# Four of eight attention gates moved into half-size products, and two sums moved between engines, in a hybrid decoder layer

## The chip, the cores and the metric

The kernel runs on one core of one Trainium2 chip. The metric is the time of one execution on the device in microseconds (us); lower is better. The core's engines run side by side and wait for each other by semaphores: TensorE (PE) multiplies matrices, VectorE (DVE) and GpSimd (POOL) do elementwise work, ScalarE (ACT) evaluates functions and copies, SyncE (SP) issues most DMAs. PE writes its products into PSUM banks, from which DVE and ACT read them.

## The reference

One decoder layer on 1024 tokens with 1024 channels, float32. A single projection of the normalized input feeds two token mixers; their outputs are projected, merged by gates, projected again, added to the input and normalized.

```python
h = rmsnorm(x, norm_g)
proj = h @ w_in
(g_q, g_k, g_v, g_gate, g_rank,
 s_q, s_k, s_v, s_gate, m_logits) = jnp.split(proj, SPLIT_IDX, axis=-1)
...
o_gla = rmsnorm(o_gla, gla_norm_g).reshape(B, T, GLA_DV) * jax.nn.silu(g_gate)
y_a = o_gla @ w_pa
o_sb = stick_breaking(s_q, s_k, s_v)          # 8 heads of 128
o_sb = o_sb.reshape(B, T, SB_WIDTH) * jax.nn.silu(s_gate)
y_b = o_sb @ w_pb
gates = jax.nn.sigmoid(m_logits + b_gate).reshape(B, T, N_BRANCH, D_MODEL)
merged = gates[:, :, 0] * y_a + gates[:, :, 1] * y_b
x = x + merged @ w_o
return rmsnorm(x, final_g)
```

Stick-breaking attention works on 128-query blocks against their causal key prefix: `log1m = log_sigmoid(-z)`, a reversed running sum over the keys gives `between`, and the weights are `exp(log_sigmoid(z) + between)`, strictly causal. The gate that this text follows most is `silu(s_gate)`, one 128-channel slice per attention head.

## The kernel before

Every float32 operand of a product is split into a high part, rounded to the fast float32 format by ACT (`split`, line 165), and a low part, the difference, by DVE (line 166). Each product is then three matmuls of 128 x 512: high by high, high by low, low by high.

The kernel runs in stages, in this order in time:

1. *Start and V* (0 to about 116 us). Normalization of x block by block (`norm_a`, `norm_b`, lines 386 to 399, with ACT's square, a small DVE instruction and POOL's power), transposes into the four quarters `hq`, and the value projections in `proj_n` (line 209). The first block's order on ACT and DVE is written out by hand (lines 424 to 455).
2. *Pairs with decay* (about 116 to 270). `Pairs` (line 69) works through a list of 28 jobs (lines 623 to 627). A job (`pair_job`, line 234) multiplies the two half matrices of hidden states by 256 columns of `w_in` with seven products of half size (Winograd's scheme) in place of eight: seven units of 12 matmuls (lines 269 to 272), the differences of the weights by POOL (lines 244 to 247), splits by ACT and DVE, and for each of four output parts an eviction. The first 22 units stand between the steps of the GLA decay (`djobs`, line 692); the next 31 between steps that load `w_pb` and `w_o`, form the differences `t_sum` on DVE and store them to `d_t` for the last stages (`tjobs`, line 729). `GLA_AT` = 53 is the number of units ahead of GLA. The jobs for GLA's q and k read the decay factors `d_e` from DRAM (line 558).
3. *GLA with pairs* (about 270 to 715). 32 steps of chunked linear attention, four units in each (line 877), the rest of the pair jobs beside them: stick-breaking q and k, the merge gates.
4. *Attention* (about 736 to 1015). 64 steps (head h, block i), lines 1088 to 1102. `scores` runs two steps ahead: three matmuls per piece, two sigmoids on ACT, a scan and a product on DVE (lines 963 and 967), a mask on POOL (line 964). `turn` transposes the block's weights on PE and splits them (near parts `at`, and `af` for the far half); `values(h, g)` multiplies them by v once for each half of the queries and evicts with the gate read from `d_sg` (lines 986 to 1004). Beside them runs a line of *filler units* (`Line`, line 55, and lines 1073 to 1081): a unit is a whole product of 24 matmuls (`proj_t`, line 197). First come 16 gate units (`gate`, line 1053: eight heads, two halves of the tokens, evicted by `silu`, line 567), then 16 units of `w_pa` (`pa`, line 1059). `SB_PLAN` says how many units run in step i before and after the transposes: one at 3, 6 and 7, so three a head; two units run ahead of the attention and six behind it.
5. *Branch output and merge* (about 1060 to 1125). 28 items (u, i) of 12 matmuls: seven half-size products (`PRODUCTS`, line 1231) of the attention output with `w_pb`. `a_merge` (line 1274) gates and adds into the merged blocks A11, A22, A12, A21. `parts` and `loads` (lines 1300 to 1313) say after which item k a weight or block is split (`his` by ACT, `los` by DVE) and loaded.
6. *Last projection* (about 1125 to 1219). 28 items (u, t) of 12 matmuls with `w_o`, the residual add, the squares and the final scaling; the loop at line 1423 goes on with the same k from 28. Its products need the sums S1 to S4 of the merged blocks (`sums`, line 1144), which POOL forms here (lines 1342 and 1438).

Outside the hand-ordered parts (`manual_schedule`) the framework's planner sets the order of instructions on each engine ahead of time by its own costs, in the order of the program where it can; each engine then runs its list in order.

Of the kernel before, what the change touches and what calls it, by code (L numbers as in the profile page):

```python
# [34 lines left out]

SB_PLAN = [(0, 0), (0, 0), (0, 0), (1, 0), (0, 0), (0, 0), (1, 0), (0, 1)]
# [9 lines left out]
GLA_AT = 53  # L46
# [57 lines left out]
def hybrid_layer(ctx: ExitStack, tc: tile.TileContext, x, norm_g, w_in, w_up, b_dec,  # L104
# [35 lines left out]
    d_s = {nm: dram_set("s" + nm, 2, [P, 2, HALF]) for nm in ("S3", "S4", "A22")}  # L140
# [220 lines left out]
    with tc.tile_pool(name="p0", bufs=3, reuse_waits="tile") as p0:  # L361
# [62 lines left out]
        with tc.manual_schedule(engines={mybir.EngineType.Activation, mybir.EngineType.DVE}):  # L424
            norm_a(0)
            (raw0, hi0, lo0), (raw1, hi1, lo1) = ws0
            norm_b(0, 0)
            norm_b(0, 1)
            xs = by_parity(xss[0])
            pts = []  # L430
            for g in range(2):
                pt = ps.tile([P, HALF], F32, tag="tr", name="tr")
                for j in range(4):
                    nc.tensor.transpose(pt[:, j * P:(j + 1) * P], xs[:, g, j], ident)
                pts.append(pt.rearrange("p (a b) -> p a b", a=4))
                nc.scalar.activation(hq[0, g][0][:, :, 0:P], pts[g], AF.Copy)
            nc.vector.tensor_copy(hi0, raw0)
            keep_warm(WARM[1])
            norm_a(1)
            for g in range(2):  # L440
                nc.vector.tensor_sub(hq[0, g][1][:, :, 0:P], pts[g], hq[0, g][0][:, :, 0:P].bitcast(F32))
            nc.vector.tensor_sub(lo0, raw0, hi0.bitcast(F32))
            nc.scalar.activation(hi1, raw1, AF.Copy)
            norm_b(1, 0)
            nc.vector.tensor_sub(lo1, raw1, hi1.bitcast(F32))
            norm_b(1, 1)
            ws0 = [w[1:] for w in ws0]
            for tb in range(1, NT):
                if tb + 1 < NT:
                    norm_a(tb + 1)  # L450
                turn_x(tb)
                if tb + 1 < NT:
                    norm_b(tb + 1)
                first_v(tb - 1)
            first_v(NT - 1)
# [136 lines left out]

    def gv_pair(h):
# [22 lines left out]
    def gla_qk(i):  # L616
# [10 lines left out]
                  [merge_pair(C_MB, i, d_gb) for i in range(4)] + [merge_pair(C_MA, 3, d_ga)], late)  # L627
# [83 lines left out]
    def t_load(k):  # L711
        wt[k] = tq.tile([P, 4, HALF], F32, tag="t", name="t")
        for two in range(2):
            rows = slice((2 * (k % 4) + two) * P, (2 * (k % 4) + two + 1) * P)
            if k < 4:
                for e in range(2):
                    nc.sync.dma_start(wt[k][:, 2 * two + e].rearrange("p (i c) -> p i c", c=P),
                                      w_pb[rows].rearrange("p (i e c) -> p e i c", e=2, c=P)[:, e])
            else:
                nc.sync.dma_start(wt[k][:, 2 * two:2 * two + 2], w_o[rows].rearrange("p (h c) -> p h c", h=2))  # L720
# [5 lines left out]
    def t_store(k):  # L726
        nc.sync.dma_start(d_t[k][:], wt[k])
# [360 lines left out]
    for s, (h, i) in enumerate(steps):  # L1088
        if i % 2 == 0 and s + 4 < len(steps):
            h2, i2 = steps[s + 4]  # L1090
            load_q(h2, i2 // 2)
        if i == 1 and h + 1 < SB_H:
            load_head(h + 1)
        if s + 2 < len(steps):
            scores(*steps[s + 2])
        st.run(SB_PLAN[i][0])
        turn(h, i)
        st.run(SB_PLAN[i][1])
        if i == 0 and s:
            values(h - 1, 1)  # L1100
        elif i == 5:
            values(h, 0)
    values(SB_H - 1, 1)
# [40 lines left out]
    def sums(pre, js, nms):  # L1144

        for j in js:
            for nm in nms:
                x1, x2_, fn, where = {"S1": ("A21", "A22", ALU.add, None), "S3": ("A11", "A21", ALU.subtract, "A21"),
                                      "S2": ("S1", "A11", ALU.subtract, "A11"),
                                      "S4": ("A12", "S2", ALU.subtract, "A12")}[nm]  # L1150
                dst = oraw[pre + where, j] if where else mo_tile("A22" if pre == "" else "N", j)
                nc.gpsimd.tensor_tensor(dst, oraw[pre + x1, j], oraw[pre + x2_, j], op=fn)
# [61 lines left out]
    sums("b", range(3), ("S1", "S3", "S2"))  # L1214
# [5 lines left out]
    sums("b", [3], ("S1", "S3", "S2"))  # L1220
# [3 lines left out]
    sums("b", ALL, ("S4",))  # L1224
# [68 lines left out]
    def y_load(n, t):  # L1293
        ys[n, t] = (sw.tile([P, D], F32, tag=("wh", "wl")[t % 2], name="y") if n == 0 else
                    py[0].tile([P, D], F32, tag="y", name="y"))
        r0 = n * HALF + t * P
        nc.sync.dma_start(ys[n, t], x2[r0:r0 + P, :])
# [14 lines left out]
    loads = {6: ("bB22", "tt"), 10: ("bT4",), 14: ("B11",), 16: ("B21", "tt"), 24: ("T2",), 26: ("T1",),  # L1312
             28: ("B22", "tt"), 34: ("S4",), 36: ("T3",), 39: ("S3", "tt"), 41: ("T4",), 43: ("A22",)}
# [16 lines left out]
    for k, it in enumerate(items):  # L1330
# [9 lines left out]
        if k >= 24:  # L1340
            y_load(0, k - 24)
            sums("", [k - 24], ("S1", "S3", "S2"))
# [15 lines left out]
    def add(n, t, J, bank):  # L1358
        nc.vector.tensor_add(ys[n, t][:, half(J)], bank, ys[n, t][:, half(J)])

    def square(n, t, J):
# [3 lines left out]
        nc.scalar.activation(junk, ys[n, t][:, half(J)], AF.Square, accum_out=ssq[:, i, J:J + 1])  # L1365
# [12 lines left out]
    def put(n, t, eng, J):  # L1378
        r0 = n * HALF + t * P
        eng.dma_start(o2[r0:r0 + P, half(J)], ys[n, t][:, half(J)])  # L1380

    def scale(n, t, J):
        y = ys[n, t][:, half(J)]
# [15 lines left out]
    def evict_c(u, t):  # L1399
# [4 lines left out]
        elif u == 5:  # L1404
            nc.vector.tensor_mul(ys[1, t][:, half(1)], ys[1, t][:, half(1)], fg[:, half(1)])
        elif u == 6:
            scale(1, t, 0)
            put(1, t, nc.sync, 0)
            nc.scalar.activation(ys[1, t][:, half(1)], ys[1, t][:, half(1)], AF.Copy, scale=pre[1, t][:, 1:2])
# [13 lines left out]
    for k, it in enumerate(items):  # L1423
# [6 lines left out]
        if 3 <= k < 7:  # L1430
            for nm in ("S4", "S3"):
                nc.sync.dma_start(d_s[nm][(k - 3) // 2][:, (k - 3) % 2], oraw[nm, k - 3])
            for nm in ("S4", "S3") if k == 6 else ():
                for j in range(4):
                    del oraw[nm, j]
        los(28 + k)
        if k < 4:
            sums("", [k], ("S4",))
# [4 lines left out]
        if k == 9:  # L1443
            mo_ctx.close()
            po.append(ctx.enter_context(tc.tile_pool(name="po", bufs=1, side="right", reuse_waits="tile")))
            py.append(ctx.enter_context(tc.tile_pool(name="py", bufs=4, reuse_waits="tile")))
            for t in range(4):
                y_load(1, t)
# [26 lines left out]
```

## Time and profile before

| What | Value |
|---|---|
| Median of three runs | 1220.27 us (1218.0 to 1220.41) |
| Profiled execution | 1220.52 us |
| Its span, first to last instruction | 1218.8 us |
| Mean granted PE clock | 0.992 |
| ACT busy | 556.1 us (46%) |
| POOL busy | 343.0 us (28%) |
| DMA moved | 249.77 MB, 205 GB/s on the mean |

Busy time is the union of an engine's instructions; a matmul's record includes the end of its pipeline, so neighbouring records overlap and the distance from start to start is its true price. "Idle before" names the instruction that the engine waited for. A granted clock of 1.00 is full speed. In the views by line, the columns are the group's count, its busy time, the mean of one in ns, and the idle time before it with what ended it. In the views by time they are start, duration, engine, line and names, and in brackets the idle time before and its cause.

### The profile page before, as it was taken

What the parts mean: (1) busy time and instruction counts of PE and PEld (TensorE: products, weight loads), DVE (VectorE), ACT (ScalarE), POOL (GpSimd) and SP (SyncE); (2) the same over time, 40 slices, a digit from 0 to 9 for tenths busy, and PEclk for the clock granted to TensorE, in tenths of its full rate; (3) what the DMA queues carried; (4) which work ended last, traced back from release to release, by engine and by line L of the source; (5) the groups of instructions that cost most, each with busy time, mean ns of one, the idle gap of its engine ahead of it and who ended that gap; (6) DMA issues with size and microseconds to landing.
All of it is one profiled execution on the core that took longest, in us unless ns stands there. A gap on an engine that the chain in (4) does not pass through costs nothing.

```text
span 1218.8 us, 17307 instructions
## 1 busy us (share of the span) xinstructions
PE 1190.8 (98%) x6087; PEld 1000.3 (82%) x6087; DVE 849.3 (70%) x1323; ACT 556.1 (46%) x1079; POOL 343.0 (28%) x319
## 2 busy tenths in 40 slices
PE   8999999999999999999999999999999999999797
PEld 8999878877888888888888887888887888788586
DVE  5575876786757667867666528777677874579876
ACT  5344663234335445444444325554456553374243
POOL 1495523142422322422423202111121111602601
PEclk9999999999999999999999999999999999999899
DMA  7544349976656646656655187545877547649562
GB/s 278 186 142 141 147 168 343 373 276 199 198 156 195 190 146 208 212 189 218 209 165 170 65 276 241 179 161 180 286 265 245 179 141 276 212 160 301 172 240 105
DMA packets 205652, 249.77 MB, mean 205 GB/s; under 512 B 12503, under 2 KB 141549, under 8 KB 203005
## 3 DMA queue, kind: packets, MB, share of 16 engines
q1 hardware_dynamic: 204988, 247.62, 61.7%
q8 instruction: 48, 0.79, 0.3%
q10 hardware_dynamic: 576, 1.05, 0.2%
q14 instruction: 40, 0.32, 0.1%
HBM read 155.30 MB, written 93.32 MB: 204 GB/s over the span
## 4 chain that ended last, share of the span: by engine, by line
PE 79%; DVE 9%; DMA 6%; ACT 3%; issue 2%; SPq 1%; POOL 0%; ACTq 0%; DVEq 0%; POOLq 0%
PE pp L270 12%; PE pp L272 12%; PE pp L271 12%; PE pp L223 8%; PE pp L204 4%; PE pp L205 4%; PE pp L206 4%; DMA f<-d_e 2%; PE av L1002 1%; PE z L955 1%; PE av L1001 1%; PE av L1000 1%; PE tr L979 1%; DMA raw<-in_w_in_dram 1%; PE z L957 1%
## 5 line engine op out<-in xcount | busy, mean ns | idle before, releaser
L964 POOL TENSOR_SCALAR_AFFINE_SELECT be<-be 128x128 f32<-128x128 f32 x64 | 40.4, 633 | 232.3 <-ACT be L960 221.1
L166 DVE TENSOR_TENSOR wl<-tt,wh 128x1024 fp32r<-128x1024 f32 x56 | 70.2, 1253 | 50.4 <-ACT wh L165 50.0
L244 POOL TENSOR_TENSOR tt<-raw 128x512 f32<-128x512 f32 x28 | 39.2, 1400 | 212.9 <-DVE wl L166 208.6
L309 DVE TENSOR_TENSOR f<-pp,f 128x512 f32<-128x512 f32 x84 | 57.7, 688 | 58.8 <-PE pp L272 58.1
L963 DVE TENSOR_TENSOR_SCAN eb<-eb,m 128x128 f32<-128x128 f32 (+3 forms) x64 | 86.5, 1353 | 9.5 <-ACT eb L959 9.5
L165 ACT ACTIVATE wh<-tt 128x1024 fp32r<-128x1024 f32 x56 | 59.3, 1059 | 68.8 <-PE pp L271 68.2
L165 ACT ACTIVATE wh<-raw 128x1024 fp32r<-128x1024 f32 x47 | 49.7, 1060 | 80.7 <-PE pp L271 39.5
L166 DVE TENSOR_TENSOR wl<-raw,wh 128x1024 fp32r<-128x1024 f32 x47 | 67.9, 1445 | 25.0 <-ACT wh L165 20.1
L276 ACT ACTIVATE f<-pp 128x512 f32<-128x512 f32 x84 | 49.6, 591 | 71.9 <-PE pp L272 70.5
L231 POOL TENSOR_TENSOR r<-r,nhalf 128x1 f32<-128x1 f32 x40 | 24.3, 607 | 188.5 <-DVE r L230 178.3
L959 ACT ACTIVATE eb<-z 128x384 f32<-128x384 f32 (+4 forms) x96 | 49.0, 511 | 36.7 <-issue 23.9
L967 DVE TENSOR_TENSOR be<-be,eb 128x128 f32<-128x128 f32 (+3 forms) x64 | 48.8, 763 | 3.2
L960 ACT ACTIVATE be<-z 128x384 f32<-128x384 f32 (+4 forms) x96 | 49.4, 515 | 0.0
L270 PE MATMUL pp<-ha11h,wh 128*128 128x512 f32 x112 | 44.8, 400 | 2.6 <-ACT wh L165 2.6
L270 PE MATMUL pp<-S3h,wh 128*128 128x512 f32 x112 | 45.0, 401 | 0.0
L270 PE MATMUL pp<-ha22h,wh 128*128 128x512 f32 x112 | 44.5, 397 | 0.2 <-DVE f L309 0.2
L270 PE MATMUL pp<-ha12h,wh 128*128 128x512 f32 x112 | 44.5, 397 | 0.0
L270 PE MATMUL pp<-S1h,wh 128*128 128x512 f32 x112 | 44.5, 397 | 0.0
L271 PE MATMUL pp<-S3l,wh 128*128 128x512 f32 x112 | 44.1, 394 | 0.0
L272 PE MATMUL pp<-S3h,wl 128*128 128x512 f32 x112 | 44.1, 394 | 0.0
L270 PE MATMUL pp<-S4h,dh 128*128 128x512 f32 x112 | 44.0, 392 | 0.0
L270 PE MATMUL pp<-S2h,wh 128*128 128x512 f32 x112 | 43.9, 392 | 0.0
(510 smaller groups left out, 4007.9 us busy)
## 6 DMA issues: line engine op xcount, KB each, us to landing
raw<-in_w_in_dram SPq DMA_DIRECT2D x31, 1024.0 KB, 6.4
d_v<-o SPq DMA_DIRECT2D x32, 256.0 KB, 3.0
d_gv<-o SPq DMA_DIRECT2D x32, 256.0 KB, 4.0
d_t<-t SPq DMA_DIRECT2D x8, 1024.0 KB, 5.5
v<-d_gv SPq DMA_DIRECT2D x32, 256.0 KB, 3.3
d_ogl<-o SPq DMA_DIRECT2D x64, 128.0 KB, 2.5
d_q<-o SPq DMA_DIRECT2D x16, 512.0 KB, 3.9
d_k<-o SPq DMA_DIRECT2D x16, 512.0 KB, 4.1
```

What stands on the lines that cost most here:

```text
L165: nc.scalar.activation(hi, src, AF.Copy)
L166: eng.tensor_sub(lo, src, hi.bitcast(F32))
L223: nc.tensor.matmul(pt[:, 0:n], *ops[kb][i], start=k == 0, stop=k == 3 * KB - 1)
L270: nc.tensor.matmul(pt, bh[:, j], ah[:, j], start=first and j == 0, stop=False, skip_group_check=True)
L271: nc.tensor.matmul(pt, bh[:, j], al[:, j], start=False, stop=False, skip_group_check=True)
L272: nc.tensor.matmul(pt, bl[:, j], ah[:, j], start=False, stop=j == 3, skip_group_check=True)
L276: nc.scalar.activation(t[nm], t[bank], AF.Copy)
L309: nc.vector.tensor_add(add, bank, add)
L959: nc.scalar.activation(om[:, osl], zt[:, 0:w], AF.Sigmoid, scale=-inv_sqrt)
L960: nc.scalar.activation(be[:, osl], zt[:, 0:w], AF.Sigmoid, scale=inv_sqrt)
L963: nc.vector.tensor_tensor_scan(rest, rest, m1[:, off:T][:, ::-1], 1.0, op0=ALU.mult, op1=ALU.max)
L967: nc.vector.tensor_mul(be[:, off:T], be[:, off:T], om[:, off + 1:T + 1])
```

## The change

There are six parts.

- The gates of heads 0 to 3 are no longer filler units. Two more pair jobs, `sg_pair(0)` and `sg_pair(1)`, form them (30 jobs in all), behind the q and k jobs; they evict by `silu` into the same `d_sg`. The filler line keeps the gates of heads 4 to 7 and all of `pa`.
- `SB_PLAN` now puts one filler unit at steps 0 and 6 of each head, ahead of the transposes. `values(h - 1, 1)` moves from step 0 to step 2, and both value products stand ahead of the step's transposes.
- `GLA_AT` goes from 53 to 70, and the weight sums of stage 2 start every 5 units instead of every 2.7; loads and stores are issued in halves.
- In the last projection the sums S1 to S4 go from POOL to DVE, one block per item at k = 28 to 40, S2 is kept in another buffer, S4 is no longer stored and read again, S3 is stored one block at a time; the splits and loads from k = 28 on are ordered anew (A12 ahead of T2).
- The residual tiles are handled as two halves, and three of the second half's are loaded at item 2, the last at item 13, instead of all at item 9.
- In the start, `norm_a(1)` moves behind the two subtractions that give the first block's low parts.

```diff
-SB_PLAN = [(0, 0), (0, 0), (0, 0), (1, 0), (0, 0), (0, 0), (1, 0), (0, 1)]
+SB_PLAN = [1, 0, 0, 0, 0, 0, 1, 0]
-GLA_AT = 53
+GLA_AT = 70
...
             keep_warm(WARM[1])
-            norm_a(1)
             for g in range(2):
                 nc.vector.tensor_sub(hq[0, g][1][:, :, 0:P], pts[g], hq[0, g][0][:, :, 0:P].bitcast(F32))
+            norm_a(1)
...
+    def sg_pair(i):
+        return pair_job(w_in, C_SG + i * DV,
+                        lambda J, n, bank, add: silu(total(bank, add), d_sg[2 * i + J][:, half(n)]))
...
-                  [merge_pair(C_MB, i, d_gb) for i in range(4)] + [merge_pair(C_MA, 3, d_ga)], late)
+                  [sg_pair(i) for i in range(2)] + [merge_pair(C_MB, i, d_gb) for i in range(4)] + [merge_pair(C_MA, 3, d_ga)], late)
...
     for k in range(8):
-        at = 27 * k // 10
-        tjobs[at].append((t_load, (k,)))
+        at = 5 * k
+        for i in range(2):
+            tjobs[at + i].append((t_load, (k, i)))
+            tjobs[at + 9 + i].append((t_store, (k, i)))
         for i in range(4):
             tjobs[at + 6 + i // 2].append((t_sum, (k, i)))
-        tjobs[at + 9].append((t_store, (k,)))
...
-    line = [gate_load(0), gate_load(1)]
-    for h in range(5):
-        line += [gate_load(h + 2), gate(h, 0), gate(h, 1)]
+    line = [gate_load(4), gate_load(5), gate_load(6), gate(4, 0), gate(4, 1)]
...
-        st.run(SB_PLAN[i][0])
-        turn(h, i)
-        st.run(SB_PLAN[i][1])
-        if i == 0 and s:
+        st.run(SB_PLAN[i])
+        if i == 2 and h:
             values(h - 1, 1)
         elif i == 5:
             values(h, 0)
+        turn(h, i)
...
-    def sums(pre, js, nms):
+    def sums(pre, js, nms, eng):
...
-                                      "S2": ("S1", "A11", ALU.subtract, "A11"),
+                                      "S2": ("S1", "A11", ALU.subtract, "A11" if pre else "A22"),
...
-                nc.gpsimd.tensor_tensor(dst, oraw[pre + x1, j], oraw[pre + x2_, j], op=fn)
+                eng.tensor_tensor(dst, oraw[pre + x1, j], oraw[pre + x2_, j], op=fn)
...
-             28: [("T2", (0,)), ("A12", 0)], 29: [("T2", (1,)), ("A12", 1)], 30: [("S2", 0), ("S2", 1), ("A12", 2)],
-             31: [("A12", 3)], 33: [("S2", 2), ("S2", 3)], 34: [("T1", (0,))], 35: [("T1", (1,))],
-             36: [("S1", 0), ("S1", 1)], 37: [("S1", 2), ("S1", 3), ("B22", (0,))], 38: [("B22", (1,))],
-             39: [("S4", (0,))], 40: [("S4", (1,))], 41: [("T3", (0,))], 42: [("T3", (1,))], 43: [("S3", (0,))],
+             28: [("A12", 0), ("A12", 1)], 29: [("A12", 2), ("A12", 3)], 30: [("T2", (0,))], 31: [("T2", (1,))],
+             32: [("S2", 0), ("S2", 1)], 33: [("S2", 2), ("S2", 3)], 34: [("T1", (0,))], 35: [("T1", (1,))],
+             36: [("S1", 0), ("S1", 1)], 37: [("S1", 2), ("S1", 3)], 38: [("B22", (0,))], 39: [("B22", (1,))],
+             40: [("S4", 0), ("S4", 1)], 41: [("S4", 2), ("S4", 3)], 42: [("T3", (0,))], 43: [("T3", (1,))],
...
+    merged = {**{28 + j: (j, ("S1", "S2")) for j in range(4)}, **{33 + j: (j, ("S4",)) for j in range(4)},
+              **{37 + j: (j, ("S3",)) for j in range(4)}}
...
     def los(k):
         for nm, js in parts.get(k, []):
             o_lo(nm, js)
+        if k in merged:
+            j, nms = merged[k]
+            sums("", [j], nms, nc.vector)
+            if nms == ("S3",):
+                nc.sync.dma_start(d_s["S3"][j // 2][:, j % 2], oraw.pop(("S3", j)))
...
         if k >= 24:
             y_load(0, k - 24)
-            sums("", [k - 24], ("S1", "S3", "S2"))
...
         los(28 + k)
-        if k < 4:
-            sums("", [k], ("S4",))
```

More of the change, by code (lines that the diff above doesn't have):

```diff
@@ L709, in hybrid_layer, with t_load @@
     tq = tq_ctx.enter_context(tc.tile_pool(name="tq", bufs=4, reuse_waits="tile"))
[L711 to L714, printed above, removed]
-            if k < 4:
[L716 to L720, printed above, removed]
+    def t_load(k, two):
+        if two == 0:
+            wt[k] = tq.tile([P, 4, HALF], F32, tag="t", name="t")
+        rows = slice((2 * (k % 4) + two) * P, (2 * (k % 4) + two + 1) * P)
+        if k < 4:
+            for e in range(2):
+                nc.sync.dma_start(wt[k][:, 2 * two + e].rearrange("p (i c) -> p i c", c=P),
+                                  w_pb[rows].rearrange("p (i e c) -> p e i c", e=2, c=P)[:, e])
+        else:
+            nc.sync.dma_start(wt[k][:, 2 * two:2 * two + 2], w_o[rows].rearrange("p (h c) -> p h c", h=2))
     def t_sum(k, i):
@@ L1213, in hybrid_layer @@
     a_load("A22", [3])
-    sums("b", range(3), ("S1", "S3", "S2"))
+    sums("b", range(3), ("S1", "S3", "S2"), nc.gpsimd)
     st.run(1)
@@ L1223, in hybrid_layer @@
     o_split("bB21", AB)
-    sums("b", ALL, ("S4",))
+    sums("b", ALL, ("S4",), nc.gpsimd)
     o_load("bT3")
```

53 lines of the change are left out of this document (28 added, 25 removed), and 3 rows, old and new, of the table parts.

## The prediction

> **What bounds the kernel now.** I read the page's busy line and the chain that ended last first, then busy time by stretch for the stages that the diff touches, then the timelines where TensorE (PE) falls short.
>
> ```profile
> span 1218.8 us, 17307 instructions
> PE 1190.8 (98%) x6087; PEld 1000.3 (82%) x6087; DVE 849.3 (70%) x1323; ACT 556.1 (46%) x1079; POOL 343.0 (28%) x319
> PE 79%; DVE 9%; DMA 6%; ACT 3%; issue 2%; SPq 1%; POOL 0%; ACTq 0%; DVEq 0%; POOLq 0%
> ```
>
> PE is the bound: 98% busy, 79% of the chain. So an edit pays by the matmuls that it removes and by the few holes in PE that it closes, and it costs where it opens new ones. In the stretches below the first numbers are the window and its length; then follow busy time (instructions) of PE, weight loads, DVE, ACT and POOL, the granted clock and DMA.
>
> ```profile
> 240.00:260.00 20.00, 17.43 (x69) 13.65 (x69) 16.75 (x19) 5.46 (x8) 6.19 (x4) 0.91 0.84 311
> 249.00:736.00 487.00, 485.72 (x2381) 399.42 (x2382) 316.10 (x645) 208.09 (x432) 138.98 (x134) 1.00 0.60 192
> 736.60:1014.60 278.00, 273.51 (x1437) 230.58 (x1437) 214.95 (x278) 144.92 (x330) 40.45 (x64) 1.00 0.61 204
> 736.60:770.00 33.40, 32.18 (x167) 26.06 (x167) 29.65 (x42) 20.14 (x49) 6.86 (x11) 1.00 0.62 206
> 875.00:910.00 35.00, 33.95 (x179) 28.34 (x179) 27.17 (x36) 17.50 (x40) 7.32 (x8) 1.00 0.80 274
> 910.00:945.00 35.00, 33.32 (x178) 28.19 (x177) 25.58 (x33) 19.38 (x43) 4.48 (x8) 1.00 0.80 267
> 945.00:980.00 35.00, 34.94 (x186) 29.73 (x185) 28.89 (x38) 18.13 (x41) 4.71 (x9) 1.00 0.52 166
> 1120.00:1140.00 20.00, 17.84 (x80) 14.43 (x78) 19.90 (x14) 7.95 (x12) 19.45 (x11) 1.00 0.68 212
> 1140.00:1160.00 20.00, 14.69 (x54) 11.20 (x53) 14.97 (x20) 6.68 (x14) 7.95 (x6) 0.74 0.40 145
> 1160.00:1180.00 20.00, 20.00 (x90) 16.57 (x89) 14.66 (x19) 9.57 (x13) 0.55 (x1) 1.00 0.78 269
> ```
>
> The attention is 736.6 to 1014.6. A full stretch of 128x512 products holds 90 matmuls in 20 us (1160 to 1180); 1120 to 1160 holds 134 of 180, and 240 to 260 holds 69. Those are the two real holes.
>
> **The change, part by part.** First the price of a matmul: the two filler units that stand alone ahead of the attention, and four transposes within it.
>
> ```profile
> 725.08 0.39 PE L204 MATMUL pp<-ha11h,wh 128*128 128x512 f32 x1
> 730.52 0.39 PE L204 MATMUL pp<-ha21h,wh 128*128 128x512 f32 x1
> 735.96 0.28 PE L955 MATMUL z<-k,q 128*128 128x256 f32 x1
> ...
> 747.24 0.60 PE L979 MATMUL tr<-ident,be 128*128 128x128 f32 x4
> ```
>
> A unit of 24 matmuls takes 5.44 us from start to start, so one matmul 0.227 us; a transpose takes at most 0.15. *Gates as pairs:* four heads had 2 units each, 8 x 24 = 192 matmuls. Two pair jobs of 7 units of 12 are 168. That removes 24 matmuls, **-5.4 us**, split into -43.5 in the attention (8 x 5.44) and +38.1 ahead of it (14 x 12 x 0.227). The added units stand in a stage where PE has 485.72 of 487 us and DVE 65%, so their adds, sigmoids, weight differences and stores lie beside PE; if that cover failed for one eviction the price would be one DVE operation of 0.7 us. The two jobs also bring eight POOL differences; POOL is at 29% there, and if each held up a DVE subtraction by the 1.1 us worked out below, 8.8 us would fall on an engine that idles 171.
>
> *Attention with two units per head.* It keeps 16 units. Without more waiting it falls to 278.0 - 43.5 = 234.5 us. What does DVE then carry?
>
> ```profile
> L570 DVE TENSOR_TENSOR o<-pp,o 128x512 f32<-128x512 f32 x15 | 10.3, 687 | 6.3 <-ACT o L569 6.3
> L166 DVE TENSOR_TENSOR wl<-raw,wh 128x1024 fp32r<-128x1024 f32 x14 | 17.1, 1224 | 16.6 <-ACT wh L165 12.4 <-PE pp L205 3.9
> L963 DVE TENSOR_TENSOR_SCAN eb<-eb,m 128x768 f32<-128x768 f32 x7 | 12.3, 1752 | 0.0
> L963 DVE TENSOR_TENSOR_SCAN eb<-eb,m 128x896 f32<-128x896 f32 x7 | 14.1, 2021 | 1.2 <-ACT eb L959 1.2
> L963 DVE TENSOR_TENSOR_SCAN eb<-eb,m 128x1024 f32<-128x1024 f32 x7 | 15.9, 2275 | 0.0
> L967 DVE TENSOR_TENSOR be<-be,eb 128x768 f32<-128x768 f32 x7 | 6.7, 959 | 0.9
> L967 DVE TENSOR_TENSOR be<-be,eb 128x896 f32<-128x896 f32 x7 | 8.2, 1172 | 0.0
> L967 DVE TENSOR_TENSOR be<-be,eb 128x1024 f32<-128x1024 f32 x7 | 8.5, 1209 | 0.0
> L166 DVE TENSOR_TENSOR atl<-tr,ath 128x256 fp32r<-128x256 f32 x14 | 5.7, 405 | 0.0
> L166 DVE TENSOR_TENSOR afl<-pp,afh 128x512 fp32r<-128x512 f32 x25 | 17.0, 681 | 0.0
> ```
>
> Eight silu products (0.69) and four weight splits (1.22) go: 214.95 - 5.5 - 4.9 = 204.6 us of DVE work. Against 234.5 that is 87%; it was 77%. PE stays the bound on average, but the slack is thin. How much PE waits at such a load, the trace bounds: at 83% (945 to 980) it lost 0.06 us of 35; at 89% (the first stretch) 1.22 of 33.4. The idle time now is 278.00 - 273.51 = 4.5, of which 2.7 stands in 875 to 945, where DMA is at 0.80 and which the edit leaves alone. At the first stretch's rate, the nearest in load, 240 us lose 8.8, and with the 2.7 that is 11.5: **+7 us** more waiting than now. The low end is 0 (the 83% stretch's rate), the high end is the imbalance under the rivals. Moving values(h-1, 1) from step 0 to step 2, and both value products ahead of the transposes, gives PE work just where DVE is slow; I book nothing for it. Its cost could be a later release of v, so a later load on SP's queue; the tile is wanted only at step 5 of the next head, more than a head (278 / 8 = 34.8 us) later, so nothing either.
>
> *GLA from unit 53 to 70, weight sums spread over 48 slots instead of 31.* The hole at 246:
>
> ```profile
> 226.11 7.99 DMA f<-d_e
> 241.65 0.69 DVE L562 SCALAR_TENSOR_TENSOR f<-pp,f 128x512 f32<-128x512 f32 x1 [3.52 <-DMA f<-d_e]
> 249.37 0.58 PE L270 MATMUL pp<-ha11h,wh 128*128 128x512 f32 x1 [2.57 <-ACT wh L165]
> 250.87 0.63 PE L272 MATMUL pp<-S3h,wl 128*128 128x512 f32 x1
> ```
>
> A 256 KB read of d_e took 8 us among the 1 MB loads and stores of the weight sums; DVE stood 3.5 us behind it, ACT's split waited for DVE's eviction, and PE for the split; then matmuls ran at half pace. The same d_e reads will now meet about half the traffic (a load and a store per 5 units, in halves, instead of per 2.7). 240 to 260 lacks 21 matmuls of a full window's 90, 4.8 us: I take **-4.5 us**; 0 if the read stays late. GLA's own first waits may stay: its loads follow the stores on SP as before.
>
> *Sums on VectorE in the last stage.* Before, with POOL idle, then with POOL beside it:
>
> ```profile
> 1113.09 0.69 DVE L1194 TENSOR_TENSOR bT4l<-raw,bT4h 128x512 fp32r<-128x512 f32 x1
> 1118.49 1.22 DVE L1194 TENSOR_TENSOR B11l<-raw,B11h 128x1024 fp32r<-128x1024 f32 x1
> 1121.34 2.31 DVE L1194 TENSOR_TENSOR B11l<-raw,B11h 128x1024 fp32r<-128x1024 f32 x1
> 1133.68 1.77 DVE L1194 TENSOR_TENSOR A12l<-A,A12h 128x512 fp32r<-128x512 f32 x1
> 1138.88 7.86 POOL L1152 TENSOR_TENSOR A<-A,A 128x512 f32<-128x512 f32 x5
> 1139.41 0.50 PE L1353 MATMUL pp<-B21h,A12l 128*128 128x512 f32 x1 [2.16 <-DVE A12l L1194]
> 1144.43 0.80 PE L1353 MATMUL pp<-B21h,A12l 128*128 128x512 f32 x1 [4.05 <-DVE A12l L1194]
> ```
>
> While POOL sums, each DVE subtraction costs 1.1 us more, DVE falls behind, and PE waits for A12's low parts; after the 4.05 us hole the granted clock is 0.74 over the window. The missing 180 - 134 = 46 matmuls are 10.4 us. After: 16 sums (S1, S2, S4, S3 of four blocks) of 0.69 on DVE, and A12 comes before T2. In item k = 28 DVE has two A12 parts and two sums, 4 x 0.69 = 2.7 us, against 12 x 0.227 = 2.72 us on PE; the same in 29 to 31. At 31 and 32 two and three evictions of 0.69 come on top, so DVE runs 4 to 5 us behind, then holds at about 2.6 per item. A12's parts are wanted four items after they are queued, S2 four, S1 four, which covers that lag; S4's last parts are queued in the item just before the one that reads them, and there up to 1 us may be late. So **-9.5 us**; between -10.4 and -5 (if each DVE operation takes 0.1 more, the lag grows by some 5 us by S4).
>
> *Start.* norm_a(1) goes behind the two low parts.
>
> ```profile
> 10.56 0.15 DVE L230 TENSOR_SCALAR r<-ssq 128x1 f32<-128x1 f32 x1 [1.64 <-ACT xs L389]
> 11.37 0.52 PE L223 MATMUL pp<-vw,ha11l 128*128 128x272 f32 x2 [1.36 <-DVE ha11l L441]
> ```
>
> DVE no longer stands 1.64 us before them; PE's wait of 1.36 goes, but the next one, for the weights' low part, then comes sooner and takes some back: **-0.8 us**, 0 to -1.4. Splitting y into halves and d_t stores into two issues costs SP 0.3 to 0.5 us each, off the path.
>
> Sum: -5.4 + 7 - 4.5 - 9.5 - 0.8 = -13.2 us. The profiled execution took 1220.5 (1.7 more than its span), the median of the runs is 1220.27; so **1207 us**.
>
> **The rivals.**
>
> *Attention waits no more than now* (+0 in place of +7), all else as above: 1200. For it: the 83% stretch; against: the first.
>
> *Half the holes stay.* DVE's lag stalls PE at S4 (-5) and d_e is still late (-2): 1214. For it: DVE runs with almost no slack in k = 28 to 40.
>
> *Slower: DVE runs behind in steps 3 to 5 of every head.* There it has three scans (6.0), three products (3.3), three near parts (some 1.2) and two far (1.4), less some 0.08 us of overlap at each, about 11.2 us; PE has scores of 768 + 896 + 1024 columns three times (3.6 at 512 per 0.227), 15 transposes (2.3) and values(h, 0) (1408 columns three times, 1.9), 7.8. The fillers stand at 0 and 6, none between. If the two steps of lookahead carry nothing, 3.4 us a head, 27 in all: 1207 - 7 + 27 = 1227. It decides from about 2.5 us a head (20 = 7 + 13.2 in all). Against it: work queued for steps 2 and 6 can slide into the gap, and the first stretch lost 1.2 us where this gives 3.4. With half of it carried, 14 in all, the time is 1214; with a quarter, 20, it is 1220, no change.
>
> A harsher form: each gap also halves the clock, as at 250.87 (0.63 for 0.39) for about ten matmuls, 2 us a head more: 1243.
>
> The Trainium skill, "TensorE: Matmul & The Clock Gate", section "Why this matters for your kernels", warns of PE gaps over about 3 us, so by the page the 3.4 us gaps would give this harsher form and gaps of 1 to 2 us would not; here a gap of 2.57 was already followed by 0.63 us matmuls, so the trace is stricter than the page.
>
> **How the numbers follow.** Forecast (1203 to 1212) 0.55; no more waiting (about 1200) 0.12; half the holes stay or half the imbalance (about 1214) 0.16; three quarters of the imbalance (1218 to 1222) 0.07; slower (1223 and up, the harsher form among it) 0.10. The range takes in the first three and leaves out the rest: 1199 to 1219. A measurement here tells about 0.2%, 2.4 us: faster 0.83, same 0.07, slower 0.10.
>
> **What would show it.** 1120 to 1160 holding nearly 180 matmuls, DVE's 128x512 subtractions at 0.69 and no POOL sum there; 240 to 260 full; the attention near 241 us with DVE at 85%; no d_e read of 8 us. Wrong if the attention takes over 250 us, if PE waits for S4's or S2's low parts, or if the weight sums only carry the hole elsewhere.

## The result and the profile after

The changed kernel takes 1212.79 us (median of four runs, 1211.37 to 1214.45) against 1220.16 beside it: a ratio of 0.9944, with an interval of 0.9927 to 0.9961. That is 7.4 us or 0.6% faster, within the range of 1199 to 1219 and 5.8 us slower than the 1207 that was forecast. The profiled execution took 1212.93 us. From the page of the changed kernel, the busy line and the shares of the chain:

```profile
PE 1185.1 (98%) x6063; PEld 995.5 (82%) x6063; DVE 858.8 (71%) x1351; ACT 565.9 (47%) x1091; POOL 331.6 (27%) x311
PE 86%; DVE 5%; ACT 3%; issue 3%; DMA 2%; SPq 0%; POOL 0%; ACTq 0%; POOLq 0%; DVEq 0%
```

The chain runs through PE for 86% of the span; it was 79%. PE has 24 matmuls fewer, as the pairs should give. The next view is busy time by stretch. Its columns are those of the prediction: window, length, then busy time (instructions) of PE, weight loads, DVE, ACT and POOL, granted clock, DMA share, GB/s. The changed kernel first:

```profile
240.00:260.00 20.00, 20.00 (x90) 16.54 (x89) 14.51 (x19) 7.98 (x13) 4.38 (x4) 1.00 0.82 281
260.00:280.00 20.00, 20.00 (x97) 16.53 (x96) 12.80 (x16) 7.93 (x12) 7.41 (x6) 1.00 0.73 238
768.10:1021.00 252.90, 238.85 (x1262) 199.72 (x1261) 204.33 (x265) 137.81 (x316) 39.88 (x64) 0.99 0.66 218
820.00:840.00 20.00, 14.52 (x62) 11.54 (x61) 13.50 (x16) 9.44 (x20) 3.51 (x5) 0.83 0.46 146
1120.00:1140.00 20.00, 20.00 (x90) 16.52 (x88) 19.20 (x26) 10.27 (x14) 0.00 (x0) 1.00 0.87 300
1140.00:1160.00 20.00, 20.00 (x90) 16.57 (x89) 19.26 (x33) 11.91 (x22) 0.00 (x0) 1.00 0.37 119
```

The same view of the kernel before, for the stretches that the prediction did not show (the attention from its first score to its last value, and a small hole):

```profile
260.00:280.00 20.00, 19.09 (x89) 15.54 (x88) 15.63 (x28) 8.51 (x14) 8.35 (x9) 1.00 0.81 257
735.96:1014.57 278.61, 274.12 (x1442) 231.19 (x1441) 215.59 (x278) 145.33 (x330) 40.45 (x64) 1.00 0.62 205
```

Both large holes are gone: 240 to 260 holds 90 matmuls instead of 69, and 1120 to 1160 holds 180 instead of 134. At 0.227 us that is 4.8 and 10.4 us. The attention gives most of it back. It has 1442 - 1262 = 180 matmuls fewer, 40.9 us, so at the old waiting it would take 237.7; it takes 252.9, **15.2 us more** than that, where the prediction had 7. PE idles 14.0 us in it (252.90 - 238.85), before it was 4.5. Of the remaining 5.7 us, an estimated 3.4 are work at a lower granted clock, 0.83 over the 20 us of 820 to 840; the other 2 are not placed. That stretch stands out, for PE is also idle in it for 5.5 us. It lies in head 1.

The account: -5.4 (pairs) + 15.2 (attention) - 4.8 - 10.4 (the two holes) - 0.9 (260 to 280) - 0.8 (1020 to 1060, where PE is busy for 40.00 us instead of 39.22) = -7.1 us; the profiled executions differ by 1220.52 - 1212.93 = 7.6.

Two views of the changed kernel show what happened in head 1. First SP's queue: the start of each DMA issue, and its duration.

```profile
800.04 0.37 SPq L1074 DMA_DIRECT2D oa11l<-d_ogl  x1
802.72 0.39 SPq L1074 DMA_DIRECT2D oa11h<-d_ogl  x1
...
806.12 0.43 SPq L1074 DMA_DIRECT2D oa12h<-d_ogl  x1
806.60 0.85 SPq L1074 DMA_DIRECT2D oa12l<-d_ogl  x1
...
808.55 0.53 SPq L907 DMA_DIRECT2D q<-d_q  x1
...
810.45 0.54 SPq L907 DMA_DIRECT2D q<-d_q  x1
```

Four loads of 1 MB, the GLA output that the `w_pa` units need (`o_dma(0)`), stand ahead of two small loads of queries: at 808.55 those of the head's blocks 6 and 7 (one load serves two blocks and is issued four steps ahead), at 810.45 the first of the next head. In the group of DMA issues between 795 and 825 the small loads take 9.5 us from issue to landing, as the median of three:

```profile
q<-d_q SPq DMA_DIRECT2D x3, 256.0 KB, 9.5
```

For the issue at 808.55 alone the same view gives 10.1 us, so the queries of blocks 6 and 7 are there at about 818.7. The timeline of PE then reads:

```profile
814.64 0.48 PE L203 MATMUL pp<-ha21h,wh 128*128 128x512 f32 x1
...
820.18 0.36 PE L960 MATMUL z<-k,q 128*128 128x448 f32 x1
...
822.61 0.50 PE L960 MATMUL z<-k,q 128*128 128x512 f32 x1 [1.06 <-ACT be L965]
...
826.43 0.52 PE L984 MATMUL tr<-ident,be 128*128 128x128 f32 x3 [1.00 <-DVE be L972]
...
830.80 0.66 PE L960 MATMUL z<-k,q 128*128 128x384 f32 x1 [3.06 <-ACT be L965]
...
833.60 0.63 PE L203 MATMUL pp<-ha21h,wh 128*128 128x512 f32 x1
```

In the program the scores of blocks 6 and 7 (from 820.18) come ahead of the head's second filler unit; here the planner has put that unit (814.64 to 820.18) before them. So the widest scans of the head follow with nothing beside them: PE waits 1.06, 1.00 and 3.06 us for work that comes out of the scans, and after the 3.06 the next matmuls run at half pace (0.66 and 0.63 us). In the kernel before, the same four loads are issued between 863 and 867, and PE is busy for all 20 us of 860 to 880. That the third filler of a head covered them there is likely, but no run tests it alone.

### The profile page after: what moved, and what is told of

Read it like the earlier page. It is cut to its first block, busy times and chain, and to the rows that moved or that the text cites. A ratio compares the mean times of both kernels' runs of the same rounds, so it can differ in the third digit from the quotient of the medians.

```text
span 1210.8 us, 17298 instructions
## 1 busy us (share of the span) xinstructions
PE 1185.1 (98%) x6063; PEld 995.5 (82%) x6063; DVE 858.8 (71%) x1351; ACT 565.9 (47%) x1091; POOL 331.6 (27%) x311
## 4 chain that ended last, share of the span: by engine, by line
PE 86%; DVE 5%; ACT 3%; issue 3%; DMA 2%; SPq 0%; POOL 0%; ACTq 0%; POOLq 0%; DVEq 0%
PE pp L269 15%; PE pp L271 14%; PE pp L270 14%; PE pp L222 8%; PE pp L203 3%; PE pp L204 3%; PE pp L205 3%; PE av L1006 1%; PE av L1007 1%; PE av L1005 1%; DVE eb L968 1%; PE xb L1369 1%; PE xb L1371 1%; PE xb L1370 1%; PE z L960 1%
## 5 line engine op out<-in xcount | busy, mean ns | idle before, releaser
L165 DVE TENSOR_TENSOR wl<-tt,wh 128x1024 fp32r<-128x1024 f32 x60 | 74.5, 1242 | 55.4 <-ACT wh L164 55.3
L308 DVE TENSOR_TENSOR f<-pp,f 128x512 f32<-128x512 f32 x90 | 62.0, 689 | 70.0 <-PE pp L271 68.8
L275 ACT ACTIVATE f<-pp 128x512 f32<-128x512 f32 x90 | 53.3, 592 | 90.0 <-PE pp L271 87.9
L164 ACT ACTIVATE wh<-tt 128x1024 fp32r<-128x1024 f32 x60 | 63.5, 1059 | 62.8 <-PE pp L270 62.3
L269 PE MATMUL pp<-ha22h,wh 128*128 128x512 f32 x120 | 47.8, 398 | 0.2 <-DVE f L308 0.2
L269 PE MATMUL pp<-ha12h,wh 128*128 128x512 f32 x120 | 47.6, 396 | 0.0
L269 PE MATMUL pp<-S1h,wh 128*128 128x512 f32 x120 | 47.5, 396 | 0.0
L244 POOL TENSOR_TENSOR tt<-raw,tt 128x512 f32<-128x512 f32 x30 | 47.3, 1578 | 0.0
L960 PE MATMUL z<-k,q 128*128 128x384 f32 (+4 forms) x96 | 39.7, 414 | 7.8 <-ACT be L965 7.2
L269 PE MATMUL pp<-S2h,wh 128*128 128x512 f32 x120 | 47.1, 392 | 0.0
```

The costliest lines, as they stand in the source:

```text
L164: nc.scalar.activation(hi, src, AF.Copy)
L165: eng.tensor_sub(lo, src, hi.bitcast(F32))
L269: nc.tensor.matmul(pt, bh[:, j], ah[:, j], start=first and j == 0, stop=False, skip_group_check=True)
L275: nc.scalar.activation(t[nm], t[bank], AF.Copy)
L308: nc.vector.tensor_add(add, bank, add)
L960: nc.tensor.matmul(zt[:, 0:n], q[:, 0], k[:, 0, ksl], start=True, stop=False)
```

## The experiments

Three theories for the attention. **A:** the 4 MB of output loads crowd SP's queue, the scores come late, and the filler is spent on that wait. **B:** VectorE's share in steps 3 to 5 of each head, the prediction's slower rival. **C:** the value products ahead of the transposes. For the last stage the rivals are GpSimd beside VectorE and the order of the splits; for the hole near 246 us, the crowded weight sums and GLA's start. Each run stands against runs of the kernel before on the same chip; their medians are 1219.77 to 1220.6, so the times compare directly.

**odma_later: the changed kernel, the first group of loads two units later in the program.**

```diff
-    line += [..., gate(7, 0), o_dma(0), gate(5, 1), pa_load(0), gate(6, 1), pa_load(1),
+    line += [..., gate(7, 0), gate(5, 1), pa_load(0), gate(6, 1), o_dma(0), pa_load(1),
```

> The changed kernel with one move: the four 1 MB loads of the GLA output's first half (o_dma(0)) are queued two filler units later, in head 2 instead of head 1. Theory A (the loads made the order around scores 6 and 7 of head 1 bad, one hole of 8 to 10 us): 1203 to 1205 us against 1212.8, and the stretch 820 to 840 holds about 105 PE instructions instead of 62. Theory B (VectorE is too loaded in steps 3 to 5 of every head): no change within 2 us, the waiting spreads over all heads. Theory C (values ahead of the transposes is what costs): no change within 2 us.

Measured: 1203.72 us (1201.96 to 1206.21), ratio 0.9864 (0.9845 to 0.9883): 9.1 us faster than the changed kernel, and 820 to 840 is full, both as theory A expected:

```profile
820.00:840.00 20.00, 19.67 (x107) 16.48 (x106) 16.36 (x26) 11.12 (x26) 1.82 (x5) 1.00 0.71 237
```

SP's queue shows how:

```profile
800.00 0.37 SPq L1074 DMA_DIRECT2D oa11l<-d_ogl  x1
802.67 0.52 SPq L907 DMA_DIRECT2D q<-d_q  x1
803.25 0.64 SPq L1074 DMA_DIRECT2D oa11h<-d_ogl  x1
809.01 0.52 SPq L907 DMA_DIRECT2D q<-d_q  x1
809.59 0.61 SPq L1074 DMA_DIRECT2D oa12h<-d_ogl  x1
```

The first of the loads is issued at the same time as in the changed kernel, 800.0. What the edit changed is that loads of queries now go between them, and that the later ones are issued later (the third at 809.59 instead of 806.12). The queries of blocks 6 and 7 are issued at 802.67 instead of 808.55, and PE takes their scores from 809.46 and 812.56 on, ahead of the filler unit, which starts at 816.44. So theory A holds: moving the loads alone brings the order on PE back. Whether the place of the queries or the distance between the large loads decides is not told apart.

**turn_then_values: the transposes ahead of the values again, the values at steps 2 and 5 as changed.**

```diff
+        turn(h, i)
         if i == 2 and h:
             values(h - 1, 1)
         elif i == 5:
             values(h, 0)
-        turn(h, i)
```

> The changed kernel with the transposes of a step ahead of its value products again; the values stay at steps 2 and 5 and the fillers at 0 and 6. Theory C (values ahead of the transposes starts them before VectorE has split the near parts, 0.7 us in each head): 1207 to 1208 us against 1212.8. Theories A and B: within 2 us of 1212.8.

Measured: 1214.82 us (1213.63 to 1215.62), ratio 0.9954 (0.9936 to 0.9972); 2 us slower than the changed kernel, if anything. Theory C falls, as far as the kernel with the crowded loads shows it.

**odma_spread: both groups of loads later.**

```diff
-    line += [..., gate(7, 0), o_dma(0), gate(5, 1), pa_load(0), gate(6, 1), pa_load(1),
-             gate(7, 1), o_dma(1), pa_load(2), pa(0, 0), pa(1, 0), pa(2, 0)]
+    line += [..., gate(7, 0), gate(5, 1), pa_load(0), gate(6, 1), o_dma(0), pa_load(1),
+             gate(7, 1), pa_load(2), pa(0, 0), pa(1, 0), o_dma(1), pa(2, 0)]
```

> The changed kernel with both groups of 4 MB output loads later: the first after gate(6, 1) as in odma_later, the second after pa(1, 0), so that neither lies close behind the other. If crowded loads that hold up the scores are what is left of the attention's loss: 1199 to 1202 us, and the 4.7 us that odma_later still lost between 860 and 880 us is mostly gone. If it is VectorE's share in steps 3 to 5: as odma_later, 1203 to 1205 us.

Measured: 1201.11 us (1199.88 to 1202.67), ratio 0.9845 (0.9828 to 0.9861): 1.5% faster than before, and the fastest kernel of this study. The attention by stretch, odma_later and then odma_spread:

```profile
768.10:1014.63 246.53, 236.98 (x1262) 199.34 (x1261) 204.08 (x265) 137.15 (x316) 39.34 (x64) 0.99 0.68 224
```

```profile
766.55:1008.18 241.63, 234.27 (x1262) 198.01 (x1261) 204.34 (x265) 136.98 (x316) 38.50 (x64) 1.00 0.69 228
```

The same 1262 matmuls take 252.9, 246.5 and 241.6 us. DVE has the same 204 us of work in all three. So 11.3 of the 15.2 us come from where two groups of loads stand on a queue; 3.9 are left. (The profile of odma_later is of its slowest run; by the medians the second group is worth 2.6 us and both together 11.7.)

**spread36: odma_spread, with a filler among the wide scans.**

```diff
-SB_PLAN = [1, 0, 0, 0, 0, 0, 1, 0]
+SB_PLAN = [0, 0, 0, 1, 0, 0, 1, 0]
```

> odma_spread (1201.1 us) with the two filler units of a head at steps 3 and 6 instead of 0 and 6, so that one stands among the wide scans. If VectorE's share in steps 3 to 5 is what the attention still loses (the prediction's rival): 1196 to 1199 us. If the lookahead already covers it: 1200 to 1203 us, and more if the filler now lacks at step 0.

Measured: 1206.98 us (1205.07 to 1209.5), ratio 0.9897 (0.9879 to 0.9914). The attention in this kernel, and one stretch of its first head:

```profile
766.66:1013.56 246.90, 236.35 (x1262) 199.95 (x1261) 205.31 (x265) 137.13 (x316) 30.12 (x64) 0.99 0.67 223
780.00:800.00 20.00, 17.89 (x100) 14.85 (x99) 19.90 (x29) 12.10 (x30) 5.76 (x7) 1.00 0.65 213
```

The attention is 5.3 us longer, and PE waits now where the filler is missing while DVE is full (19.90 of 20). If steps 3 to 5 were short of PE work, a filler there should have helped. Theory B is not what the attention loses, as far as this one placement shows.

**gates_only: the kernel before with the gates edit alone** (the two pair jobs, the shorter line of fillers, the plan, and the values ahead of the transposes; the weight sums, the last stage and the start as before).

```diff
-SB_PLAN = [(0, 0), (0, 0), (0, 0), (1, 0), (0, 0), (0, 0), (1, 0), (0, 1)]
+SB_PLAN = [1, 0, 0, 0, 0, 0, 1, 0]
...
+                  [sg_pair(i) for i in range(2)] + ...
...
-    line = [gate_load(0), gate_load(1)]
-    for h in range(5):
-        line += [gate_load(h + 2), gate(h, 0), gate(h, 1)]
+    line = [gate_load(4), gate_load(5), gate_load(6), gate(4, 0), gate(4, 1)]
```

> The kernel before with the gates edit alone (four gates as pairs ahead of the attention, two filler units per head, values ahead of the transposes); weight sums, last stage and start as before. If the pairs save 5.4 us and the attention gives back about 15 us, as in the accounts by stage of the changed kernel: 1227 to 1231 us, and the hole near head 1's scores 6 and 7 is there again. If the attention gives back 7 us as the prediction had it: 1220 to 1223 us. If the attention's loss in the changed kernel came from the other edits: about 1215 us.

Measured: 1230.68 us (1230.08 to 1231.75), ratio 1.0084 (1.0069 to 1.0099): **10.8 us slower**. Its attention and its head 1:

```profile
772.27:1027.58 255.31, 240.59 (x1262) 201.07 (x1261) 204.40 (x265) 137.63 (x316) 39.44 (x64) 0.98 0.60 201
820.00:840.00 20.00, 14.37 (x64) 11.51 (x63) 12.35 (x15) 9.27 (x20) 2.59 (x4) 0.84 0.61 205
```

The hole in head 1 is the edit's own. The part of the change that gave it its name made the kernel slower; the other parts paid for it.

**no_gates: the changed kernel with that edit undone** (the values at their old steps behind the transposes, too).

```diff
-SB_PLAN = [1, 0, 0, 0, 0, 0, 1, 0]
+SB_PLAN = [(0, 0), (0, 0), (0, 0), (1, 0), (0, 0), (0, 0), (1, 0), (0, 1)]
...
-                  [sg_pair(i) for i in range(2)] + ...
...
-    line = [gate_load(4), gate_load(5), gate_load(6), gate(4, 0), gate(4, 1)]
+    line = [gate_load(0), gate_load(1)]
+    for h in range(5):
+        line += [gate_load(h + 2), gate(h, 0), gate(h, 1)]
```

> The changed kernel with the gates edit undone (all eight gates as filler units, values behind the transposes at their old steps); weight sums, last stage and start stay changed. If the edits add up, the changed kernel's 1212.8 less the 10.8 us that gates_only lost: 1201 to 1204 us, and the attention at about 278 us. If the gates edit is worth the predicted -5.4 + 7 us: about 1211 us. If the wide spread of the weight sums needs the pairs' longer stage: over 1206 us with a hole in GLA.

Measured: 1206.74 us (1206.61 to 1207.76), ratio 0.989 (0.9875 to 0.9904). That is the third expectation's time, so the edits do not simply add up; its hole, though, is not inside GLA but where GLA ends and the attention begins:

```profile
715.00:735.00 20.00, 18.77 (x95) 14.88 (x92) 10.59 (x29) 6.66 (x21) 3.59 (x10) 1.00 0.71 206
735.00:745.00 10.00, 8.11 (x39) 5.43 (x39) 8.73 (x14) 6.98 (x18) 1.72 (x5) 1.00 0.91 353
```

Without the two gate pairs there are 28 x 7 = 196 units, and GLA, which starts after unit 70 and takes 32 x 4, would need 198. So its end has no other work beside it: 3.1 us of these 30 are idle, and 0.4 of the same stretch in the changed kernel (750 to 780).

**no_gates57: the same with GLA as far from the end as in the changed kernel.**

```diff
-GLA_AT = 70
+GLA_AT = 57
...
-        at = 5 * k
+        at = 35 * k // 10
```

> no_gates (1206.7 us) with GLA from unit 57 and one weight sum block per 3.5 units, as far from the end of the pairs as GLA stands in the changed kernel. If no_gates lost its last 4 us where GLA's end meets the attention (715 to 745 us), and the edits otherwise add up: 1201 to 1204 us. If the sums at 3.5 units bring the late read of d_e back: 1206 to 1209 us with a hole near 246 us. If the gates edit costs the changed kernel only the 6 us that no_gates showed: 1206 to 1207 us with no such hole.

Measured: 1204.62 us (1203.31 to 1207.49), ratio 0.9878 (0.9861 to 0.9894), close above the first expectation's 1204. The same stretch:

```profile
715.00:745.00 30.00, 28.67 (x137) 22.80 (x137) 17.09 (x23) 15.02 (x34) 4.21 (x11) 1.00 0.89 291
```

So beside the other edits the gates edit costs 1212.79 - 1204.62 = 8.2 us as it was made, and with the loads spread it gains 1204.62 - 1201.11 = 3.5; the runs of these three kernels do not overlap.

**gla53 and gla70_27: the weight sums crowded again, with GLA from unit 53 and from unit 70.** Both put the loads and stores of a block at 2.7 units; gla53 also moves GLA.

```diff
-        at = 5 * k
+        at = 27 * k // 10
```

> The changed kernel with the weight sums again every 2.7 units and GLA from unit 53 (loads and stores still in halves). If the crowd of weight loads and stores made the d_e reads late: 1217 to 1219 us, a hole of some 5 us near 246 back. If the size of one load or store was the cause, halves cure it: 1212 to 1214 us.

> The changed kernel with GLA still from unit 70, but the weight sums crowded at one block per 2.7 units as before (gla53 had both back). If the crowding of 1 MB loads and stores makes the late read of d_e: the hole near 246 us is there again, 1216 to 1219 us as gla53. If GLA's place at unit 53 made it: 1212 to 1214 us.

Measured: 1218.38 us (1216.87 to 1220.16), ratio 0.9987 (0.9978 to 0.9997), and 1218.87 us (1215.53 to 1223.86), ratio 0.9986 (0.9974 to 0.9999). The timeline of gla53, DVE and PE:

```profile
242.53 0.69 DVE L561 SCALAR_TENSOR_TENSOR f<-pp,f 128x512 f32<-128x512 f32 x1 [4.08 <-DMA f<-d_e]
250.21 0.50 PE L269 MATMUL pp<-ha11h,wh 128*128 128x512 f32 x1 [3.90 <-ACT wh L164]
```

In gla70_27 the same two waits are 3.94 and 3.93 us. The chain of the prediction, read of `d_e`, DVE, ACT, PE, is back in both; GLA's place makes no difference to it, and loads and stores in halves do not cure it. The spread of the weight sums closes the hole, and it is worth 5.6 to 6.1 us.

One link of that chain reads differently from the prediction. These are pieces of the chain of work in the kernel before:

```profile
234.19 0.70 DVE f L562
234.91 0.33 SPq L563
...
235.29 6.27 DMA f<-d_e
```

The read of 8 us, issued at 226.11, lands at 234.10. DVE's wait of 3.52 us ends with the next read, which SP issues only at 235.29, behind a store of DVE's product (line 563) that stood ahead of it on the queue. So the last read is late more than it is slow: in gla53 and gla70_27 no read of `d_e` takes over 6.3 us, but the last is issued at 236.06 and 237.85; in the changed kernel the last two are issued from 228.68 on, and DVE waits 0.2 us in all for the reads instead of 5.9. Nor did the traffic halve: between 205 and 240 DMA moved 363 GB/s before and 312 in the changed kernel.

**sums_pool, before_order, before_sums: the last stage's two edits apart.** sums_pool is the changed kernel with S1 to S4 on GpSimd again; before_order is the kernel before with only the order of the splits changed; before_sums is the kernel before with only the engine changed.

```diff
-            sums("", [j], nms, nc.vector)
+            sums("", [j], nms, nc.gpsimd)
```

> The changed kernel with the sums S1 to S4 of the last projection on GpSimd again, in the new order. If GpSimd beside VectorE was the cause of the holes at 1120 to 1160 (each VectorE subtraction 1.1 us longer): 1220 to 1226 us, 128x512 subtractions at 1.7 us there, holes back. If the order of A12 and T2 was the cause: 1212 to 1215 us.

```diff
-             28: [("T2", (0,)), ("A12", 0)], 29: [("T2", (1,)), ("A12", 1)], 30: [("S2", 0), ("S2", 1), ("A12", 2)],
-             31: [("A12", 3)], 33: [("S2", 2), ("S2", 3)], ...
+             28: [("A12", 0), ("A12", 1)], 29: [("A12", 2), ("A12", 3)], 30: [("T2", (0,))], 31: [("T2", (1,))],
+             32: [("S2", 0), ("S2", 1)], 33: [("S2", 2), ("S2", 3)], ...
```

> The kernel before with one edit: in the last stage the four A12 blocks are split ahead of T2; the sums stay on GpSimd. If the order made the holes between 1120 and 1160 us: about 1210 us (1208 to 1213), few waits for A12's low parts, subtractions still at 1.7 us. If GpSimd beside VectorE made them, as the prediction had it: 1218 to 1221 us, the holes still there.

```diff
-                nc.gpsimd.tensor_tensor(dst, oraw[pre + x1, j], oraw[pre + x2_, j], op=fn)
+                (nc.gpsimd if pre else nc.vector).tensor_tensor(dst, oraw[pre + x1, j], oraw[pre + x2_, j], op=fn)
```

> The kernel before with one edit: the last stage's sums on VectorE instead of GpSimd, at their old places and in the old order of the splits. If GpSimd beside VectorE made the holes between 1120 and 1160 us: 1210 to 1212 us, subtractions at 0.7 us. If the order made them: VectorE's own load is about as large as before (some 11 us of sums more, some 11 us of lengthened subtractions less), PE still waits for A12's low parts, 1217 to 1222 us.

Measured: sums_pool 1213.41 us (1210.37 to 1217.83), ratio 0.995 (0.9934 to 0.9967), which cannot be told from the changed kernel, although each A12 subtraction takes 1778 ns in it; 1120 to 1160 holds 172 matmuls. before_order 1209.04 us (1208.07 to 1209.77), ratio 0.9905 (0.989 to 0.992). before_sums 1216.77 us (1215.17 to 1218.23), ratio 0.997 (0.9958 to 0.9983). The stretches of before_order, with A12's subtraction in the groups by line (count, then busy time and mean in ns):

```profile
1120.00:1140.00 20.00, 20.00 (x90) 16.41 (x89) 19.93 (x15) 6.60 (x10) 19.45 (x12) 1.00 0.59 187
1140.00:1160.00 20.00, 19.60 (x87) 15.83 (x86) 19.77 (x28) 13.01 (x22) 6.67 (x4) 1.00 0.74 245
L1194 DVE TENSOR_TENSOR A12l<-A,A12h 128x512 fp32r<-128x512 f32 x4 | 6.9, 1776 | 0.0
```

and of before_sums, with PE's wait in the list of waits (total, times, longest):

```profile
1120.00:1140.00 20.00, 17.16 (x74) 13.23 (x72) 19.62 (x27) 6.92 (x10) 0.00 (x0) 1.00 0.73 244
1140.00:1160.00 20.00, 18.36 (x68) 14.56 (x69) 14.10 (x26) 10.40 (x19) 0.00 (x0) 0.83 0.39 132
L1194 DVE TENSOR_TENSOR A12l<-A,A12h 128x512 fp32r<-128x512 f32 x4 | 2.7, 684 | 0.0
PE pp L1353 <- DVE A12l L1194: 4.5, 4, 1.6
```

This is the sharpest pair of the study. In before_order GpSimd sums beside DVE and each A12 subtraction takes 1776 ns, and the 40 us hold 177 of 180 matmuls. In before_sums GpSimd does nothing there, a subtraction takes 684 ns, and PE still waits for A12's low parts: 142 of 180. The order decides: with the old one the holes stand on either engine, with the new one they are closed on either. before_sums does not free DVE, for the sums themselves now stand on it, so it does not show what GpSimd's presence alone costs. DVE is full from 1120 to 1140 in both (19.93 and 19.62 of 20 us); what counts is whether the part that PE needs next is at the head of its queue.

## Why the prediction was right, and where it was not

The time lies within the range of 1199 to 1219, but just above the forecast's own 1203 to 1212, in the band at 1214 that had a chance of 0.16. And by its own sign ("wrong if the attention takes over 250 us") the prediction was wrong about the attention, which took 252.9.

- **Gates as pairs, -5.4:** right; 24 matmuls fewer on the page. The added units cost what was said: the attention starts 32.1 us later (768.10 against 735.96), and 38.1 - 4.8 - 0.9 is 32.4.
- **Attention, +7:** the direction was right, the size was not. It measured 15.2 in the changed kernel and, by its time against the kernel before plus the 5.4 saved, 16.2 in gates_only. The step that failed is the rate taken from the first stretch, 1.2 us in 33 for DVE's share, together with "2.7 stands in 875 to 945, where DMA is at 0.80 and which the edit leaves alone". The edit moved those loads: with eight units fewer ahead of them in the line, `o_dma(0)` came in head 1 at 800 us, and ahead of the queries of its last blocks. The prediction followed v's loads past SP's queue and not these. With the queue in order the attention takes 241.6 us with DVE at 85% (204.34 of 241.63), which is what the prediction said one would see: 3.9 us of more waiting, inside its bounds. So the forecast of 1207 left out a collision; the kernel without it takes 1201.
- **The hole at 246, -4.5:** 4.8, and 0.9 more just behind it. gla53 and gla70_27 show that the crowd on SP's queue makes it, as told; but the sign "no d_e read of 8 us" went by the wrong read, and "about half the traffic" did not come. What changed is when the last reads are issued.
- **Last stage, -9.5:** 10.4. The size was right and the reason wrong. "While POOL sums, each DVE subtraction costs 1.1 us more" is true, but it is not what costs the time: the sums moved to DVE in the old order gave 3.1 us, and the order alone, which the prediction only named beside it, gave 10.8. The feared lateness of S4 did not come; 1120 to 1160 is full.
- **Start, -0.8:** not to be seen. PE is busy for 35.8 of the first 40 us before and for 35.9 after; the wait of 1.36 for the low part became one of 1.28 for the weights, as the prediction feared.
- **The rivals:** the slower one was told as DVE's imbalance, 1227. The gates edit alone did come out at 1230.7, by another mechanism; spread36 speaks against the imbalance. "Half the holes stay" gave nearly the right time, 1214, for a reason that did not occur: both holes were closed.

That the time fell within the range is in part luck: one term was 8 us too small, the holes gave 1 to 3 us more than booked, and the range of 20 us was wide enough for the difference.

The last 3.9 us can be placed only in part. These are PE's largest waits in the attention of odma_spread (total, times, longest), and below them the largest of the kernel before:

```profile
PE av L1006 <- DVE atl L165: 3.2, 7, 0.5
PE z L960 <- ACT be L965: 3.0, 5, 1.2
```

```profile
PE tr L979 <- DVE atl L166: 2.1, 2, 1.5
PE z L955 <- ACT be L960: 0.9, 3, 0.3
```

All waits of such a list come to 7.0 us in odma_spread and to 4.2 before, so 2.8 of the 3.9 are waits. Seven of the eight heads lose half a us where the value products follow close on the last transposes that they need and wait for DVE's split of these. The place of the values in the program does not make it: turn_then_values, which puts them behind the transposes of their step again, has the same seven waits, 3.5 us in all. Whether it would pay with the loads spread was not tried.

## What to carry to other kernels

When filler work is taken out of a stage, look for what the removed units kept apart: large loads that ride in the same line move forward with it. Here a small load behind four of them landed after 10.1 us, and the order of work on TensorE came out worse. When a full engine makes another wait, first ask what stands ahead of the needed instruction in its queue; here the order of four subtractions gave 11 us, and taking GpSimd from beside them, with its sums put on VectorE, gave 3. Test each part of a joint change alone: here one lost 11 us, one gained 11, and one, undone from the whole, was worth 6.

## What was not expected of the hardware

The granted clock fell behind waits that were shorter than the prediction reckoned with, and not each time. The changed kernel and sums_pool run the same instructions in head 1. Each fence holds two rows of PE's timeline and the stretch they stand in, for the changed kernel first:

```profile
810.76 0.50 PE L1005 MATMUL av<-ath,v 128*128 128x512 f32 x1 [0.75 <-ACT ath L164]
812.26 0.50 PE L1006 MATMUL av<-atl,v 128*128 128x512 f32 x1 [1.00 <-DVE atl L165]
810.00:815.00 5.00, 3.25 (x21) 2.79 (x21) 4.60 (x7) 1.83 (x6) 0.00 (x0) 1.00 1.04 392
```

```profile
810.73 0.50 PE L1005 MATMUL av<-ath,v 128*128 128x512 f32 x1 [0.75 <-ACT ath L164]
812.23 0.79 PE L1006 MATMUL av<-atl,v 128*128 128x512 f32 x1 [1.00 <-DVE atl L165]
810.00:815.00 5.00, 3.27 (x10) 2.76 (x11) 3.84 (x5) 1.34 (x4) 0.00 (x0) 0.72 1.03 388
```

The same two waits, 0.75 and 1.00 us, stand at the same place; behind them the clock stays at 1.00 in one and falls to 0.72 in the other, where the second product takes 0.79 us instead of 0.50. No single gap is near the 2.57 us of the prediction. The Trainium skill, "TensorE: Matmul & The Clock Gate", section "Why this matters for your kernels", warns of idle gaps over about 3 us; the 3.06 us gap of the changed kernel agrees with it (0.63 us for a 128x512 matmul behind it, 0.39 at full pace). The shorter ones lie outside that warning, and the clock fell behind them in one of the two cases. What decides between the cases was not found. The runs of sums_pool go from 1210.37 us at a granted clock of 0.997 to 1217.83 at 0.991; that falls like this one make the difference is not shown.
